# A two-block start pipeline with three gates streamed through one PSUM pool, and pools that wait per tile

## The chip, the cores and the metric

The kernel runs on one core of a Trainium2 chip. The metric is the device time of one execution in microseconds (us); a lower time is better. Before the change, three runs gave 1739.57, 1734.92 and 1736.54 us, the median is 1736.54 us. One further execution was taken with the hardware profiler: it took 1736.99 us, of which the profile's span covers 1735.1 us.

The engines of the core are called PE (matrix multiply), DVE (vector), ACT (scalar, with activation functions) and POOL (general purpose); SP only issues DMAs here. Each engine works through its own instructions in program order. PE writes its results into PSUM, a small memory of eight banks; everything else lives in SBUF.

## What is computed

One layer of a hybrid diffusion backbone, for 640 tokens (128 context and 512 latent tokens), 1024 channels wide:

```python
h    = rms_norm(x) * (1 + scale) + shift        # scale, shift = silu(c) @ w_ada
proj = h @ w_in                                 # q k v | conv b c x | z | xbc | dt | 3 gates
attn = blocked_attention(rope(norm(q)), keys, vals) @ w_attn_o
conv = (conv_bg * dwconv(conv_cg * conv_x, conv_w)) @ w_conv_o
dt   = softplus(dt_raw + dt_bias)
ssd  = ssd_scan(silu(dwconv(xbc)), dt, a) ... @ w_ssd_o
...
y    = x + g1 * ((sigmoid(gate_0) * attn + sigmoid(gate_1) * conv + sigmoid(gate_2) * ssd) @ w_merge)
y    = y + g2 * swiglu(modulated_norm(y))
```

The kernel keeps float32 accuracy with matrix units that take a shorter format: each operand is split into a high part and a low part, and a product is three matmuls, high by high, high by low and low by high.

## The kernel before

**Tiling.** Channels lie on the 128 partitions, so the normalised activations `h` are 8 blocks of 128 x 640, each with a high and a low tile. A matmul takes 320 tokens (half of them) at a time. Weights come in pieces of 128 x 1024 or 128 x 512 float32 (`wr`, three buffers) by DMAs that SP issues. ACT rounds each piece to its high part (`wh`, L166) and DVE subtracts to get the low part (`wl`, L167); `h` is split in the same way.

**Two ways to multiply.** The plain way, `fblock` (L311), costs 3 matmuls for each block of `h`, each half and each 128 output channels: 96 for the 256 output channels of one gate. The other way, `sunit` with `product` (L250), is a seven-product scheme over sums of weight quarters and of `h` quarters: 84 matmuls for the same work, but POOL has to sum weights (`ws`, L227 to L230), DVE has to form sums of `h` quarters once (`sum_forms`, tiles `T`), and DVE and ACT combine the seven products as they come (`uv`, `g`).

**Stages.** The program has these stages, each with a PSUM pool of its own that is opened by `psum(n)`. Here `n` is the count of two-bank accumulators `acc`, and the other banks are single-bank tiles `mx`.

- *Start*, `psum(2)`: load `x`, sum squares (L409), reciprocal root mean square on one row (L359, L346, L348), then a loop over the 8 blocks of `h`. For each block: `products` (16 small matmuls of `silu(c)` with an `ada` weight piece, L419; ACT copies one half of the result as `ms`, L421, and DVE adds the other, L422), `factors` (two tiny matmuls, L428, then shift `mod` and scale `A` on DVE, L429 and L431), `modulated` (the normalised block `hf`, 512 columns on ACT, L435, 128 on DVE, L436, and the high part by an ACT cast, L437), `scaled` (x times the reciprocal root, L440), `low` (L443), and `stream` (12 plain matmuls of the first gate on this block). The loop is a five-step pipeline: step n does products of block n, factors of block n-2, low parts of block n-3 and the gate's matmuls of block n-5. The order of PE, ACT and DVE is the written one here (`manual_schedule`); elsewhere a scheduler orders instructions by priority.
- *Projections and convolution*, `psum(1)`: the four sums of `h` quarters, one plain gate (`plain_gate`, 96 matmuls), the dt matmuls (L499) with which `decays` begins, then four `conv_units` of three seven-product units each, with one seven-product gate after units 1, 2 and 3. `decays` is a generator whose vector work is handed out in pieces between the units: softplus as a polynomial on 128 x 320 tiles (L522 to L529), each step a multiply (L524) and an add (L525).
- *Attention*, `psum(1)` and then `psum(3)` for the scores (L759); *SSD*, `psum(2)`; *merge and FFN*, `psum(4)`, whose second norm starts with a sum of squares `ssq` (L1017) and ten one-column matmuls (L359); *output side of the FFN*, `psum(0)`, which begins with seven-product units again.

**Pools.** When a pool closes and another opens over the same memory, the first writers of the new pool wait until all users of the old one are done.

Of the kernel before, what the change touches and what calls it, by code (L numbers as in the profile page):

```python
# [85 lines left out]
def layer_kernel(  # L86
# [15 lines left out]
    const = ctx.enter_context(tc.tile_pool(name="const", bufs=1))  # L102
    hpool = ctx.enter_context(tc.tile_pool(name="hpool", bufs=2 * KB))
    wp = ctx.enter_context(tc.tile_pool(name="wp", bufs=2))
    fs = ctx.enter_context(tc.tile_pool(name="fs", bufs=8))
# [272 lines left out]
    with tc.tile_pool(name="start", bufs=10) as sp, psum(2):  # L378
# [16 lines left out]
        for k in ORDER[1:3]:  # L395
            modulation_load(k)
# [17 lines left out]
        def products(k):  # L414

            pm, w = mx(), aws.pop(k)
            for i in range(KB):
                q = 32 * (i % 4)
                pe.matmul(pm[q:q + 32, 256 * (i // 4):256 * (i // 4) + 256], cz[:, i, :], w[:, i, :], start=True, stop=True)  # L419
            rows1[k] = sp.tile([P, 256], F32, tag="ms", name=nm("ms"), bufs=4)  # L420
            act.copy(rows1[k], pm[:, :256])  # L421
            dve.tensor_tensor(rows1[k], rows1[k], pm[:, 256:], op=add)  # L422
# [9 lines left out]

        def modulated(k):
# [3 lines left out]
            act.copy(h[k].hi, hf[k])  # L437
# [4 lines left out]
        def low(k):  # L442
            dve.tensor_tensor(h[k].lo, hf[k], f32(h[k].hi), op=sub)  # L443

        def stream(n):
            k = ORDER[n]
            for m in range(2):
                fblock(early[m], we, m, h, k + 1, first=n == 0, last=n == KB - 1, start=k)
# [3 lines left out]
        with tc.manual_schedule(engines={e.engine for e in (pe, act, dve)}):  # L452
            rs = rstd(sq, TOKBLKS, sp)
            for n in range(KB + 5):
                if n + 3 < KB:
                    modulation_load(ORDER[n + 3])
                if n == 0:
                    raws = [qraw(w_gt[EARLY], a) for a in range(2)]
                if n < KB:
                    products(ORDER[n])  # L460
                if n == 0:
                    rr = rowcast(rs, TOKBLKS, sp)
                    early = [acc() for _ in range(2)]
# [1056 lines left out]
```

## Time and profile before

| what | value |
|---|---|
| three runs, median | 1736.54 us |
| the profiled execution | 1736.99 us |
| its span | 1735.1 us |
| granted PE clock, mean over the span | 0.991 |
| PE busy / idle in the span | 1689.1 us / 46.0 us |
| DVE, ACT, POOL busy | 1306.2, 764.8, 297.7 us |

The timeline lists, for each run of like instructions: when it starts in the span, how long it lasts, the engine, the source line, the operation, output tile from input tiles, shapes, and the count; in brackets behind it stand the engine's idle time just before and what ended it. The view of windows gives busy time by engine in a stretch, and then the granted PE clock (1.00 is full, 0.50 is half), the share of DMA time and the rate. PE's matmuls overlap each other a little, so the distance from one start to the next is the cost of one, rather than the listed length.

### The profile page before, as it was taken

The page shows a single profiled execution, that of the slowest core. Times are in us where ns is not written, and L with a number is a line of the kernel's source. Part 1 is how long each engine was busy: PE and PEld are TensorE (multiplying, and loading weights), DVE is VectorE, ACT ScalarE, POOL GpSimd, SP SyncE. Part 2 cuts the span into 40 slices and gives each one's busy share as a digit, 9 for nine tenths or more (in the row PEclk, how much of TensorE's full clock was granted, in tenths as well). Part 3 has the DMA queues.
Part 4 walks back from the last instruction along what each step waited for, and adds up shares of the span by engine and source line. Part 5 has one row for each costly group of instructions (what it writes and reads, how often), then busy time and mean ns, then how long its engine had stood idle before and what let it go on. Part 6 is the DMA issues. An engine that isn't in the chain of part 4 may idle for free.

```text
span 1735.1 us, 30084 instructions
## 1 busy us (share of the span) xinstructions
PE 1689.1 (97%) x11814; PEld 1644.3 (95%) x11814; DVE 1306.2 (75%) x2353; ACT 764.8 (44%) x1437; POOL 297.7 (17%) x261
## 2 busy tenths in 40 slices
PE   5899999999999999999999999999999999999998
PEld 4889999999999999999999999999999999999998
DVE  5799776786646888878877588995578666767888
ACT  4434443565555565555555332312355332424442
POOL 0244451110001111111011000000001231324432
PEclk8999999999999999999999999999999999999999
DMA  8223234211243534454444588773441222222222
GB/s 338 86 82 99 91 123 146 76 44 53 83 125 107 166 123 139 142 161 135 140 150 137 182 284 296 257 231 103 158 145 49 88 73 86 74 86 87 72 74 98
DMA packets 126974, 225.05 MB, mean 130 GB/s; under 512 B 9200, under 2 KB 69488, under 8 KB 125808
## 3 DMA queue, kind: packets, MB, share of 16 engines
q1 hardware_dynamic: 126832, 223.12, 40.1%
q8 instruction: 93, 1.52, 0.4%
q14 instruction: 49, 0.40, 0.1%
HBM read 199.43 MB, written 23.66 MB: 129 GB/s over the span
## 4 chain that ended last, share of the span: by engine, by line
PE 81%; DVE 7%; issue 2%; POOL 1%; ACT 1%; DMA 0%; DVEq 0%; POOLq 0%; ACTq 0%
PE acc L311 41%; PE mx L250 20%; PE mx L311 6%; DVE wl L167 2%; PE acc L1258 2%; PE mx L993 2%; PE mx L945 2%; PE mx L999 1%; PE acc L759 1%; PE mx L298 1%; PE mx L299 1%; PE mx L297 1%; PE mx L971 1%; PE mx L922 1%; PE acc L775 1%
## 5 line engine op out<-in xcount | busy, mean ns | idle before, releaser
L311 PE MATMUL acc<-h,wh 128*128 128x320 f32 x2560 | 488.7, 313 | 1.7 <-DVE h L443 1.0
L311 PEld LDWEIGHTS acc<-h,wh 128*128 128x128 f32 x2560 | 401.0, 189 | 5.1 <-issue 2.7
L166 ACT CAST wh<-wr 128x1024 fp32r<-128x1024 f32 (+2 forms) x224 | 216.7, 969 | 320.7 <-PE acc L311 146.3
L167 DVE TENSOR_TENSOR wl<-wr,wh 128x1024 fp32r<-128x1024 f32 (+2 forms) x224 | 272.8, 1219 | 95.4 <-ACT wh L166 94.1
L311 PE MATMUL acc<-h,wl 128*128 128x320 f32 x1280 | 293.0, 310 | 0.0
L311 PEld LDWEIGHTS acc<-h,wl 128*128 128x128 f32 x1280 | 214.9, 189 | 0.0
L250 PE MATMUL mx<-h,wh 128*128 128x320 f32 x848 | 189.6, 311 | 3.0 <-DVE g L162 3.0
L250 PE MATMUL mx<-s,wh 128*128 128x320 f32 x720 | 160.0, 310 | 0.2 <-DVE s L162 0.2
L311 PE MATMUL acc<-s,wh 128*128 128x320 f32 x768 | 152.7, 309 | 0.0
L967 ACT ACTIVATE ex<-rw,nlc 128x128 f32<-128x128 f32 x320 | 102.7, 394 | 107.3 <-DVE M L969 60.3
L250 PEld LDWEIGHTS mx<-h,wh 128*128 128x128 f32 x848 | 142.4, 189 | 4.1 <-DVE g L162 3.3
L166 ACT CAST wh<-ws 128x512 fp32r<-128x512 f32 (+3 forms) x114 | 84.7, 747 | 132.0 <-PE mx L250 63.8
L961 POOL TENSOR_SCALAR_AFFINE_SELECT rw<-rw 128x512 f32<-128x512 f32 x80 | 57.8, 745 | 463.4 <-DMA rw<-D_a 458.3
L250 PE MATMUL mx<-h,wl 128*128 128x320 f32 x424 | 131.6, 310 | 0.0
L311 PEld LDWEIGHTS acc<-s,wh 128*128 128x128 f32 x768 | 123.1, 188 | 0.3 <-ACT s L169 0.3
L250 PEld LDWEIGHTS mx<-s,wh 128*128 128x128 f32 x720 | 120.7, 188 | 0.7 <-DVE s L162 0.7
L250 PE MATMUL mx<-T,wh 128*128 128x320 f32 x480 | 107.9, 313 | 6.8 <-DVE uv L162 6.8
L167 DVE TENSOR_TENSOR wl<-ws,wh 128x512 fp32r<-128x512 f32 (+3 forms) x114 | 105.7, 928 | 10.7 <-ACT wh L166 9.5
L250 PE MATMUL mx<-s,wl 128*128 128x320 f32 x360 | 111.4, 309 | 0.0
L311 PE MATMUL acc<-s,wl 128*128 128x320 f32 x384 | 97.8, 309 | 0.0
L311 PE MATMUL mx<-s,wh 128*128 128x320 f32 x512 | 95.9, 309 | 0.0
L1117 DVE CUSTOM_DVE_ANT_0 jk<-aw,cr 128x512 f32<-128x512 f32 x128 | 88.2, 689 | 4.5 <-DMA aw<-in_ada_dram 2.1
(306 smaller groups left out, 3268.3 us busy)
## 6 DMA issues: line engine op xcount, KB each, us to landing
wr<-in_w_f_dram SPq DMA_DIRECT2D x60, 512.0 KB, 3.8
rw<-D_a SPq DMA_DIRECT2D x40, 512.0 KB, 3.9
aw<-in_ada_dram SPq DMA_DIRECT2D x64, 256.0 KB, 4.1
wr<-in_w_gt_dram SPq DMA_DIRECT2D x24, 512.0 KB, 3.9
wr<-in_w_cv_dram SPq DMA_DIRECT2D x24, 512.0 KB, 3.9
aw<-in_ada_dram SPq DMA_DIRECT2D x8, 1024.0 KB, 12.6
wr<-in_w_x_dram SPq DMA_DIRECT2D x16, 512.0 KB, 4.0
wr<-in_w_bc_dram SPq DMA_DIRECT2D x16, 512.0 KB, 3.7
```

What stands on the lines that cost most here:

```text
L166: act.copy(hi_t, src)
L167: dve.tensor_tensor(lo_t, src, f32(hi_t), op=sub)
L250: pe.matmul(out, y, z, start=not more and i == 0 and j == 0, stop=i == n - 1 and j == 2, skip_group_check=True)
L297: pe.matmul(out, l.hi, r.hi, start=start, stop=False)
L298: pe.matmul(out, l.hi, r.lo, start=False, stop=False)
L311: pe.matmul(bank(ps, e), x, y[:, e * HT:(e + 1) * HT], start=first and i == start and j == 0, stop=last and i == k - 1 and j == 2)
L945: pe.matmul(ps[:, d0 * GW:d1 * GW], xb[:, c, GW:], xw.pop(c)[:, d0:d1, :], start=True, stop=True)
L961: pool.affine_select(rw[:, d], rw[:, d], pattern=[[0, HPG], [1 - 2 * d, P]], compare_op=ALU.is_ge, fill=-1e4, base=0, channel_multiplier=2 ...
L967: act.activation(ex[:, d, r, :], rw[:, d, r, :], AF.Exp, bias=nlc[:, c, j:j + 1])
L993: pe.matmul(pf[:, q * P:(q + 1) * P], pv[:, c, d, m * P:(m + 1) * P], b["C"][:, tok], start=True, stop=True)
L1117: dve.tensor_tensor_reduce(jk, aw, cr[:, s, :], 0.5, 0.0, op0=mult, op1=add, accum_out=mp[:, q, m, s:s + 1])
L1258: pe.matmul(ps[:, e, :HT], y, z, start=i == 0 and j == 0, stop=i == KB - 1 and j == 2)
```

## The change

It does these things.

1. Every SBUF and PSUM pool is opened with `reuse_waits="tile"`: a new tile waits for the users of its own bytes alone.
2. The pool `psum(1)` is opened once, ahead of the start, and serves the start and the projections. The first gate accumulates in four `mx` tiles, and `products` and `factors` use the other two.
3. The start loop is a two-step pipeline. Step n does the products of block n, the high and low parts of block n-1, `scaled` of block n, the first gate's matmuls of block n-2, and then `factors` of block n, with `hf` in it. The first gate's weights are split in step 1, a second gate's in step 5, and 7 of the 8 blocks of that gate's first half run in steps 7 and 8.
4. `products` accumulates both halves in PSUM, so the eight adds of L422 go.
5. Two gates instead of one are done the plain way, by `streamed`, in the written order, interleaved with the sums of `h` quarters; the written order now reaches to the dt matmuls. Two seven-product gates are left, after units 1 and 3. That is 96 matmuls in place of 84.
6. The two first pieces of gate weights are loaded ahead of the third `ada` piece, and the second gate's pieces in step 1, ahead of `ada` pieces 6 to 8.
7. The polynomial is written so that each step is one `scalar_tensor_tensor`: 9 vector instructions instead of 16.

```diff
-    hpool = ctx.enter_context(tc.tile_pool(name="hpool", bufs=2 * KB))
+    hpool = ctx.enter_context(tc.tile_pool(name="hpool", bufs=2 * KB, reuse_waits="tile"))
...
-        with tc.tile_pool(name=nm("psum"), bufs=2, space=bass.MemoryType.PSUM) as p:
+        with tc.tile_pool(name=nm("psum"), bufs=2, space=bass.MemoryType.PSUM, reuse_waits="tile") as p:
...
-    EARLY, PLAIN, SPARE = GATES[0], GATES[1:2], GATES[5:]
+    EARLY, PLAIN, SPARE = GATES[0], GATES[1:3], GATES[5:]
...
-                pe.matmul(pm[q:q + 32, 256 * (i // 4):256 * (i // 4) + 256], cz[:, i, :], w[:, i, :], start=True, stop=True)
+                pe.matmul(pm[q:q + 32, :256], cz[:, i, :], w[:, i, :], start=i < 4, stop=i >= 4, skip_group_check=True)
             rows1[k] = sp.tile([P, 256], F32, tag="ms", name=nm("ms"), bufs=4)
             act.copy(rows1[k], pm[:, :256])
-            dve.tensor_tensor(rows1[k], rows1[k], pm[:, 256:], op=add)
...
+        rs = rstd(sq, TOKBLKS, sp)
+        early = [(mx(), mx()) for _ in range(2)]
+        fill = None
+        for n in range(KB + 2):
+            if n + 3 < KB:
+                modulation_load(ORDER[n + 3])
+            if n < KB:
+                products(ORDER[n])
+            if n == 0:
+                rr = rowcast(rs, TOKBLKS, sp)
+            if 1 <= n <= KB:
+                parts_of(ORDER[n - 1])
+            if n == 1:
+                we = Quarters([qsplit(raw) for raw in raws])
+                raws = [qraw(w_gt[PLAIN[0]], a) for a in range(2)]
+            if n == 5:
+                wf, fill = Quarters([qsplit(raw) for raw in raws]), acc()
+                raws = [qraw(w_gt[PLAIN[1]], a) for a in range(2)]
+            if n < KB:
+                scaled(ORDER[n])
+            if n >= 2:
+                for m in range(2):
+                    streamed(early[m], we, m, n - 2)
+            if n < KB:
+                factors(ORDER[n])
+            if n == KB - 1:
+                streamed(fill, wf, 0, *range(4))
+            if n == KB:
+                streamed(fill, wf, 0, *range(4, 7))
...
-        dve.tensor_scalar(q, s2, 2.0 / (2 * n + 1), 2.0 / (2 * n - 1), op0=mult, op1=add)
-        for j in range(n - 2, -1, -1):
-            dve.tensor_tensor(q, q, s2, op=mult)
-            dve.tensor_scalar(q, q, 2.0 / (2 * j + 1), None, op0=add)
+        dve.tensor_scalar(q, s2, 2.0 / (2 * n + 1), None, op0=mult)
+        for j in range(n - 1, 0, -1):
+            dve.scalar_tensor_tensor(q, q, 2.0 / (2 * j + 1), s2, op0=add, op1=mult)
             if j % 2 == 0:
                 yield
-        dve.tensor_tensor(q, q, u, op=mult)
+        dve.scalar_tensor_tensor(q, q, 2.0, u, op0=add, op1=mult)
...
+        sums(0)
+        for m in range(2):
+            gate_out(EARLY, m, early[m])
+        streamed(fill, wf, 0, KB - 1)
+        gate_out(PLAIN[0], 0, hv2(fill))
+        sums(1)
+        w3 = Quarters([qsplit(raw) for raw in raws])
+        ps = mx(), mx()
+        streamed(ps, wf, 1, *range(KB))
+        sums(2)
+        gate_out(PLAIN[0], 1, ps)
+        sums(3)
+        for m in range(2):
+            ps = mx(), mx()
+            streamed(ps, w3, m, *range(KB))
+            gate_out(PLAIN[1], m, ps)
+        written.close()
...
-            if i:
+            if i % 2:
                 gate_unit(*todo.pop(0))
```

Three places show how this moves instructions on the engines. A row gives the line, the operation, the output tile from its input tiles (with running numbers) and the shape.

The first place is ACT in the middle of the start loop, around the first split of gate weights. `ms` is the copied result of `products`, `hf` a normalised block, `h` its high part, `wh` the high part of a weight piece. Before:

```order
L421 COPY ms_203<-mx_194 128x256
L421 COPY ms_227<-mx_218 128x256
L421 COPY ms_242<-mx_233 128x256
L435 ACTIVATE hf_104<-s_121,mod_74,A_76 128x512
L437 CAST h_85<-hf_104 128x640
L421 COPY ms_265<-mx_256 128x256
L435 ACTIVATE hf_108<-s_125,mod_74,A_76 128x512
L437 CAST h_93<-hf_108 128x640
L166 CAST wh_278<-wr_190 128x1024
L166 CAST wh_282<-wr_192 128x1024
L421 COPY ms_297<-mx_288 128x256
```

After:

```order
L440 COPY ms_207<-mx_198 128x256
L451 ACTIVATE hf_104<-s_121,mod_74,A_76 128x512
L440 COPY ms_236<-mx_227 128x256
L458 CAST h_85<-hf_104 128x640
L166 CAST wh_240<-wr_143 128x1024
L166 CAST wh_244<-wr_145 128x1024
L451 ACTIVATE hf_108<-s_125,mod_74,A_76 128x512
L440 COPY ms_271<-mx_262 128x256
L458 CAST h_93<-hf_108 128x640
L451 ACTIVATE hf_105<-s_122,mod_74,A_76 128x512
```

The first block's `hf` now comes ahead of the second block's `ms`, the cast of a block comes after the next block's `ms`, and the weight casts follow the first block's cast instead of the second's.

The second place is PE between the last `factors` of the loop and the next group of matmuls. `acc` and `mx` are PSUM tiles, `h` with an odd number is a high part and with an even number a low part, `wh` and `wl` are the weight's parts. Before, the first gate's matmuls of the last two blocks in its stream end the loop, and the plain gate follows in a new pool:

```order
L311 MATMUL acc_215<-h_91,wl_279 128x320 x2
L311 MATMUL acc_214<-h_99,wh_282 128x320 x2
L311 MATMUL acc_214<-h_100,wh_282 128x320 x2
L311 MATMUL acc_214<-h_99,wl_283 128x320 x2
L311 MATMUL acc_215<-h_99,wh_282 128x320 x2
L311 MATMUL acc_215<-h_100,wh_282 128x320 x2
L311 MATMUL acc_215<-h_99,wl_283 128x320 x2
L311 MATMUL mx_600<-h_85,wh_589 128x320
L311 MATMUL mx_601<-h_85,wh_589 128x320
```

After:

```order
L446 MATMUL mx_470<-comb,ms_453 128x2 x2
L311 MATMUL acc_386<-h_85,wh_378 128x320 x2
L311 MATMUL acc_386<-h_86,wh_378 128x320 x2
L311 MATMUL acc_386<-h_85,wl_379 128x320 x2
L311 MATMUL acc_386<-h_93,wh_382 128x320 x2
L311 MATMUL acc_386<-h_94,wh_382 128x320 x2
L311 MATMUL acc_386<-h_93,wl_383 128x320 x2
L311 MATMUL acc_386<-h_87,wh_378 128x320 x2
L311 MATMUL acc_386<-h_88,wh_378 128x320 x2
L311 MATMUL acc_386<-h_87,wl_379 128x320 x2
L311 MATMUL acc_386<-h_95,wh_382 128x320 x2
```

Directly behind the last `factors` there are now matmuls of the second gate on blocks whose parts are early ones, in an accumulator of the same pool.

The third place is PE where the pool `psum(4)` of the merge and FFN gives way to `psum(0)`: `acc_14838` is the last accumulator of the old pool, `mx_14925` and `mx_14926` (after: `mx_14902` and `mx_14903`) are the first two products of the first seven-product unit in the new one, and a bracket names the engines whose semaphores the instruction waits for. Before:

```order
L1258 MATMUL acc_14838<-h_14535,wl_14779 128x320
L250 MATMUL mx_14925<-h_14162,wh_14903 128x320 [waits DVE_49]
L250 MATMUL mx_14925<-h_14162,wh_14903 128x320
L250 MATMUL mx_14925<-h_14162,wl_14904 128x320
L250 MATMUL mx_14925<-h_14174,wh_14903 128x320 x2
...
L250 MATMUL mx_14925<-h_14198,wl_14904 128x320
L250 MATMUL mx_14926<-s_14595,wh_14903 128x320 x2
L250 MATMUL mx_14926<-s_14595,wl_14904 128x320
```

After:

```order
L250 MATMUL mx_14902<-h_14139,wh_14880 128x320 [waits DVE_49]
L250 MATMUL mx_14902<-h_14139,wh_14880 128x320
L250 MATMUL mx_14902<-h_14139,wl_14881 128x320
L250 MATMUL mx_14902<-h_14151,wh_14880 128x320 x2
...
L250 MATMUL mx_14902<-h_14175,wl_14881 128x320
L250 MATMUL mx_14903<-s_14572,wh_14880 128x320 [waits DVE_49]
L250 MATMUL mx_14903<-s_14572,wh_14880 128x320
L250 MATMUL mx_14903<-s_14572,wl_14881 128x320
```

No matmul has moved here, but the waits have: before, the first product waits once, for the last user of the old pool, and the second product has no wait of its own. After, the first product waits for the DVE instructions that read the accumulator whose bytes it takes, the last but one of the old pool, and the second has a wait of its own, for the readers of the last one.

More of the change, by code (lines that the diff above doesn't have):

```diff
@@ L369, in layer_kernel, with streamed, gate_out @@
     GATES = [(br, mt) for br in range(3) for mt in range(4)]
-    EARLY, PLAIN, SPARE = GATES[0], GATES[1:2], GATES[5:]
+    EARLY, PLAIN, SPARE = GATES[0], GATES[1:3], GATES[5:]
     normed = ExitStack()
-    hf_pool = normed.enter_context(tc.tile_pool(name="normed", bufs=KB))
+    hf_pool = normed.enter_context(tc.tile_pool(name="normed", bufs=KB, reuse_waits="tile"))
     hf = [slot(hf_pool, "hf") for _ in range(KB)]
     wdt = hf_pool.tile([P, KB, 64], F32, name="wdt", bufs=1)
-    with tc.tile_pool(name="start", bufs=10) as sp, psum(2):
+    banks, written = ExitStack(), ExitStack()
+    banks.enter_context(psum(1))
+    def streamed(ps, w, m, *ns):
+        for n in ns:
+            k = ORDER[n]
+            fblock(ps, w, m, h, k + 1, first=n == 0, last=n == KB - 1, start=k)
+    def gate_out(x, m, ps):
+        g = slot()
+        for e in range(2):
+            act.activation(g[:, e * HT:(e + 1) * HT], bank(ps, e), AF.Tanh, scale=0.5)
+        nc.sync.dma_start(D_g[KB * x[0] + 2 * x[1] + m], g)
+    with tc.tile_pool(name="start", bufs=10, reuse_waits="tile") as sp:
         cf = sp.tile([P, KB, 2], F32, name="cf", bufs=1)
@@ L394, in layer_kernel @@
         nc.sync.dma_start(par, cols)
-        for k in ORDER[1:3]:
-            modulation_load(k)
+        modulation_load(ORDER[1])
+        raws = [qraw(w_gt[EARLY], a) for a in range(2)]
+        modulation_load(ORDER[2])
         th = sp.tile([P, KB, 2], F32, name="cth", bufs=1)
@@ L436, in modulated, with parts_of @@
             dve.tensor_scalar(hf[k][:, c:c + m], xs[k][:, c:c + m], A1[:, k, 1:2], mod1[:, k, 0, 1:2], op0=mult, op1=add)
-            act.copy(h[k].hi, hf[k])
         def scaled(k):
             dve.tensor_tensor(xs[k], xs[k], rr, op=mult)
-        def low(k):
+        def parts_of(k):
+            act.copy(h[k].hi, hf[k])
             dve.tensor_tensor(h[k].lo, hf[k], f32(h[k].hi), op=sub)
[L445 to L448, printed above, removed]
@@ L452, in layer_kernel @@
[L452 to L463, printed above, removed]
-                if 2 <= n < KB + 2:
-                    factors(ORDER[n - 2])
-                    modulated(ORDER[n - 2])
-                if 1 <= n <= KB:
-                    scaled(ORDER[n - 1])
-                if 3 <= n < KB + 3:
-                    low(ORDER[n - 3])
-                if n == 3:
-                    we = Quarters([qsplit(raw) for raw in raws])
-                if n >= 5:
-                    stream(n - 5)
+        written.enter_context(tc.manual_schedule(engines={e.engine for e in (pe, act, dve)}))
@@ L642, in conv_units, with sums @@
             yield
[L644 to L646 removed]
+        def sums(i):
+            sum_forms(forms, halves, lambda: half_op(pj, "T", 16), (i,))
+        sums(0)
[15 more added lines that the diff above has]
+        written.close()
         todo = [x for x in GATES if x not in [EARLY] + PLAIN + SPARE]
```

40 lines of the change are left out of this document (12 added, 28 removed).

## The prediction

> **What bounds the kernel now.** I read the busy times first, then the chain that ended last, then PE's waits, then PE's timeline around each long wait, and last the windows.
>
> ```profile
> span 1735.1 us, 30084 instructions
> PE 1689.1 (97%) x11814; PEld 1644.3 (95%) x11814; DVE 1306.2 (75%) x2353; ACT 764.8 (44%) x1437; POOL 297.7 (17%) x261
> PE 81%; DVE 7%; issue 2%; POOL 1%; ACT 1%; DMA 0%; DVEq 0%; POOLq 0%; ACTq 0%
> ```
>
> PE is busy for 97% of the span and holds 81% of the chain. It idles 1735.1 - 1689.1 = 46.0 us. So a change that leaves the matmuls alone can win at most these 46 us, and what PE loses at half clock. The first row of PE's waits is the longest.
>
> ```profile
> PE acc L359 <- DVE sq L409: 13.6, 1, 13.6
> ```
>
> 13.6 us pass before the first matmul, and the change touches none of what leads there. The other 32 us lie in the start loop, in the convolution, and where pools close.
>
> ```profile
> 27.97 1.94 PE L419 MATMUL mx<-aw,cz 128*32 128x256 f32 x16 [3.43 <-DMA aw<-in_ada_dram]
> 40.18 1.07 PE L419 MATMUL mx<-aw,cz 128*32 128x256 f32 x16
> 58.27 1.43 PE L311 MATMUL mx<-h,wh 128*128 128x320 f32 x4 [3.68 <-ACT s L478]
> 61.63 1.27 PE L311 MATMUL mx<-h,wh 128*128 128x320 f32 x4
> 73.16 0.75 PE L311 MATMUL mx<-h,wh 128*128 128x320 f32 x4
> 74.04 0.75 PE L311 MATMUL mx<-h,wh 128*128 128x320 f32 x4
> 75.01 4.53 PE L499 MATMUL mx<-hf,wdt 128*64 128x320 f32 x32
> ...
> 26.20:36.45 10.25, 8.48 (x51) 6.01 (x52) 8.84 (x17) 6.82 (x10) 0.00 (x0) 0.50 1.01 407
> 36.45:56.90 20.45, 17.14 (x135) 15.06 (x133) 14.21 (x27) 10.92 (x17) 6.08 (x4) 1.00 0.33 111
> 56.90:63.80 6.90, 5.53 (x21) 5.53 (x22) 6.90 (x11) 3.04 (x6) 2.94 (x2) 0.51 0.45 163
> ```
>
> PE has two prices. From 73.16 to 74.04 six matmuls of 320 columns take 0.88 us, 0.147 each; from 58.27 to 61.63 twelve take 3.36, 0.28 each. The windows give the reason: the granted clock is 1.00 in the one place and 0.51 in the other. A wait of over 3 us here is followed by several us at half clock (3.43 ahead of 27.97, 3.68 ahead of 58.27), so such a wait costs more than its idle time.
>
> **The start, part 1: how fast the new loop can go.** With blocks two steps apart, a block's `hf` follows the block before through ACT and DVE in turn. These rows give the pace (an instruction's cost is the distance to the next start on its engine, about 0.1 us under its length).
>
> ```profile
> 41.32 0.37 ACT L421 COPY ms<-mx 128x256 f32<-128x256 f32 x1 [0.64 <-PE mx L419]
> 42.52 0.82 ACT L435 ACTIVATE hf<-s,mod,A 128x512 f32<-128x512 f32 x1 [0.67 <-DVE A L431]
> 43.23 1.03 ACT L166 CAST wh<-wr 128x1024 fp32r<-128x1024 f32 x1
> 44.17 0.72 ACT L437 CAST h<-hf 128x640 fp32r<-128x640 f32 x1
> ...
> 19.91 0.82 DVE L348 COPY s<-acc 128x640 f32<-128x640 f32 x1 [1.25 <-PE acc L346]
> 42.06 0.15 DVE L429 TENSOR_TENSOR mod<-mx,par 128x4 f32<-128x4 f32 x1
> 42.25 0.23 DVE L431 TENSOR_SCALAR A<-mod,par 128x2 f32<-128x2 f32 x1
> 42.78 0.82 DVE L440 TENSOR_TENSOR s<-s,s 128x640 f32<-128x640 f32 x1
> 43.51 0.82 DVE L443 TENSOR_TENSOR h<-hf,h 128x640 fp32r<-128x640 f32 x1
> 44.30 1.23 DVE L167 TENSOR_TENSOR wl<-wr,wh 128x1024 fp32r<-128x1024 f32 x1
> ```
>
> One block takes `hf` 0.71, the next `ms` 0.27, the cast 0.72, the low part 0.74, `scaled` 0.74, `mod` 0.20, `A` 0.27: 3.67 us with hand-overs. The splits in steps 1 and 5 put two low parts of 1.23 us in front of `scaled`: 6.13 there. The first `hf` can begin after the row at 19.91, one `scaled`, `mod` and `A`: about 22.0. Then 28.1, 31.8, 35.5, 39.1, 45.3, 48.9, 52.6 for the last. PE is to do 1.07 (products) + 12 x 0.147 + 0.5 = 3.33 us per block, which fits in 3.67 at full clock. Eight `ms` adds of DVE are gone. They lay beside PE's work, so I price them at nothing beyond this chain.
>
> **The start, part 2: the matmuls behind it.** The last `factors` needs the `ms` that follows the seventh `hf` on ACT: 48.9 + 0.71 + 0.27, and 0.5 for itself, about 50.5. From there PE has in written order 24 + 12 + 18 + 12 + 6 + 48 + 96 = 216 matmuls (second gate on four blocks, first gate, second gate on three more, first gate, the rest of the second, and the third gate): 216 x 0.147 = 31.7. The cover holds: the last low part is out at 52.6 + 2.2 = 54.8, when PE still has fill until 58. So dt starts at about 82.3, against 75.01 before. But one seven-product gate is gone from the later program, 84 x 0.147 = 12.3 us of PE, and 75.01 + 12.3 = 87.3. The 3.68 us wait with its half clock goes too; that is inside this difference, as are the twelve matmuls more (1.8 us). **The gain is 4.7 to 5.0 at full clock throughout.** The splits leave PE 2.3 to 2.8 us idle in two blocks, and the first blocks run cold as before; I take off 1.5 us and use **3.2 us, from 0 to 5**.
>
> The DMAs moved ahead: the first gate's weights put the third `ada` piece back by 1 MB, at 407 GB/s 2.6 us, to some 23 us, and its user comes at 28. The second gate's weights wait on SP for the split's buffer, and `ada` pieces 6 to 8 are queued behind. The split ends near 27, 1 MB later is 29.3, and the pieces follow each 2.6 us: 32, 34.5, 37, for users after 39. That hides all of it, by over 2 us. The four sums of `h` quarters on DVE now come beside 150 plain matmuls, 22 us; the window from 56.90 shows DVE full for 6.9 us with them, so they fit.
>
> [...]
>
> **The convolution.**
>
> ```profile
> 116.25 0.57 PE L250 MATMUL mx<-T,wh 128*128 128x320 f32 x2 [2.37 <-DVE uv L162]
> 132.28 0.90 PE L250 MATMUL mx<-T,wh 128*128 128x320 f32 x2 [3.35 <-DVE uv L162]
> ...
> 100.00:120.00 20.00, 17.63 (x120) 17.21 (x119) 19.90 (x30) 7.42 (x10) 6.17 (x4) 1.00 0.23 79
> 132.00:135.40 3.40, 3.12 (x12) 3.12 (x13) 3.33 (x8) 0.00 (x0) 0.04 (x1) 0.50 0.46 159
> ...
> 112.22 1.50 DVE L524 TENSOR_TENSOR s<-s,s 128x320 f32<-128x320 f32 x1
> 113.75 0.33 DVE L525 TENSOR_SCALAR s<-s 128x320 f32<-128x320 f32 x1
> ```
>
> Here DVE is the bound: 19.90 of 20.00 us busy, and PE waits for it 2.37 and 3.35 us, then runs 3.4 us at half clock, which costs 1.5. Seven polynomial steps fewer take 0.33 to 1.5 us each off DVE, 2 to 10 us in all. Yet most of those dropped come after the second wait. Ahead of the two waits one step each goes, because each piece between two yields is handed out at a fixed place and the first piece keeps its three steps. The steps that last 1.5 are those beside POOL's weight sums; a shorter list may only move POOL's time to another step. I take **1.0 us, from -1 to 7.2** (2.37 + 3.35 + 1.5, both waits and the clock).
>
> **The pool ends.** Work per pool end: what PE waits for now, and what its new wait is for.
>
> ```profile
> 340.47 0.55 PE L759 MATMUL acc<-kh,qh 128*128 128x320 f32 x2 [1.41 <-ACT raw L713]
> 503.38 0.85 PE L311 MATMUL acc<-h,wh 128*128 128x320 f32 x4 [0.46 <-ACT s L816]
> 994.48 1.30 PE L359 MATMUL acc<-cst,ssq 128*128 128x1 f32 x10 [1.45 <-ACT s L570]
> 1343.27 0.56 PE L250 MATMUL mx<-h,wh 128*128 128x320 f32 x2 [3.00 <-DVE g L162]
> ...
> 995.60:999.00 3.40, 3.40 (x15) 3.40 (x15) 3.01 (x5) 3.21 (x6) 1.67 (x1) 0.50 0.90 300
> 1343.80:1347.20 3.40, 3.40 (x15) 3.40 (x14) 0.00 (x0) 0.42 (x1) 1.72 (x2) 0.50 0.34 131
> ...
> 338.62 0.82 DVE L167 TENSOR_TENSOR ql<-acc,qh 128x640 fp32r<-128x640 f32 x1
> 991.49 1.75 DVE L1017 TENSOR_TENSOR ssq<-ssq,s 128x640 f32<-128x640 f32 x2
> 1337.07 0.87 DVE L162 SCALAR_TENSOR_TENSOR g<-g,acc 128x320 f32<-128x320 f32 x2
> 1342.75 0.47 DVE L162 SCALAR_TENSOR_TENSOR g<-g,acc 128x320 f32<-128x320 f32 x1
> ```
>
> - 340.47: the wait for `raw` on ACT goes; the low part of q, which the scores need, is done at 338.62 + 0.82 = 339.44. Gain **1.0**.
> - 503.38: the wait for `s` on ACT goes, nothing else is late: **0.4**.
> - 994.48: the wait for `s` on ACT goes; `ssq` is done at 993.24, so the start moves 1.2 earlier. The 1.45 us idle and 1.30 us of tiny matmuls are followed by a window at 0.50, where 3.4 us do the work of 1.7. With the idle time gone I count 1.5 of it: **2.7, or 1.2** if the clock falls all the same.
> - 1343.27: PE stands still from 1340.27. The first product, 12 matmuls or 1.76 us, now waits only for a reader that ended at 1337.94, so it runs inside the gap. The second waits until 1342.75 + 0.47 = 1343.22; about 1.2 us idle remains. The window after it was at 0.50: 1.5 more. **3.3, or 1.8** without the clock.
>
> Together **7.4, from 4.4 to 9**. All later users of these pools have waits that are no later than now, so I price the rest at nothing.
>
> **The sum**, against the profiled execution's own time of 1736.99 (0.03% above the median of the runs): 1736.99 - 3.2 - 1.0 - 7.4 = **1725.4 us**, 0.67% faster. A measurement of this kernel can tell about 0.3% from no change, 5.2 us.
>
> **The rivals.**
>
> - *DVE's relief in the convolution counts in full.* For it speaks DVE's 19.90 of 20.00; against it, that few steps go ahead of the waits. Both waits and their clock go: 6.2 us more, 1719.2. Chance 0.17.
> - *The new start gives nothing, or the pools' waits don't fall.* The first: the clock stays low until 36 as before, and the loop wins no time: 1736.99 - 1.0 - 7.4 = 1728.6, less if the clock falls at pool ends all the same: 1731.6. The second, that the option doesn't do what it says: the bracket on the second product speaks against it; then 1736.99 - 4.2 = 1732.8. Chance together 0.22, of which 0.06 lies under 1731.8.
> - *Half clock through the whole start loop: slower.* At half clock a block costs PE 1.93 + 12 x 0.28 + 1.0 = 6.3 us, not 3.67. From the moment PE is the slower of the two, there are no gaps, and the window at 58 to 63 shows that dense work takes some 5 us to come back to full clock; but if the products' small matmuls (32 columns of weights each) don't count as work, it never comes back in the loop. Six blocks by 2.6 is 15.8, and 18 fill matmuls at 0.13 more is 2.4: the start loses 18.2 - 4.7 = 13.5, all else wins 8.4, and the time is 1742. It decides at a granted clock under 3.33 / 3.67 = 0.91 from 26 to 50 us. Against it: the window from 36.45 has 1.00 with the same mix of matmuls. Chance 0.08.
>
> **How the numbers follow.** The forecast has the remaining 0.53. Its own range is 1721 to 1729. Faster by over 0.3% (under 1731.8): forecast 0.53, first rival 0.17, and 0.06 of the second, 0.76 in all. Within 0.3%: 0.16 of the second and 0.03 of the third, 0.19. Slower by over 0.3%: 0.05 of the third. The range runs from 1716, the low ends of all terms, to 1734, above the second rival; it leaves out the third rival and the tails of the terms.
>
> **What would show it.** Right: dt's row at 82 to 84 us; `hf` of the last block near 52; no row with a wait of over 3 us between 26 and 82; PE's clock 1.00 from 36 on; the scores' row without a wait of ACT; the first product of the last pool directly behind the accumulators, and the second behind 1.2 us idle; windows at 1.00 after both pool ends. Wrong: dt later than 87, a window at 0.50 inside the loop, the two `uv` waits as long as now or longer, or gone. A new wait on DVE for the sums of `h` quarters, or on SP's queue for an `ada` piece, would break the cover named in the start.

## The result and the profile after

| kernel | median of the runs | lowest to highest | ratio, 95% interval |
|---|---|---|---|
| before | 1736.6 us (4 runs) | 1734.9 to 1739.6 | |
| changed | 1724.5 us (4 runs) | 1723.1 to 1725.6 | 0.993 [0.9914, 0.9945] |

The changed kernel is 0.7% faster; the forecast was 1725.4 us. The profiled execution took 1725.58 us with a span of 1723.8 us, 11.3 less than before. These lines of the page of the changed kernel answer to those shown of before:

```profile
span 1723.8 us, 30050 instructions
PE 1688.1 (98%) x11826; PEld 1643.1 (95%) x11826; DVE 1295.2 (75%) x2330; ACT 762.5 (44%) x1437; POOL 289.9 (17%) x257
PE 84%; DVE 10%; issue 3%; ACT 1%; DMA 1%; POOL 1%; SPq 0%; DVEq 0%; POOLq 0%; ACTq 0%
```

PE's busy time has hardly moved, though there are 12 matmuls more. Most of the 11.3 us came out of PE's idle time: 1723.8 - 1688.1 = 35.7 us, where it was 46.0. The waits of PE in the changed kernel that bear on the change (each row names the waiting engine and tile, what it waited for, the total, how many times, and the longest):

```profile
PE acc L362 <- DVE sq L428: 13.5, 1, 13.5
PE mx L446 <- ACT ms L440: 4.5, 2, 2.6
PE mx L250 <- DVE uv L162: 4.4, 3, 2.8
PE mx L250 <- DVE g L162: 1.3, 1, 1.3
PE acc L297 <- DVE pTl L167: 1.0, 1, 1.0
```

The wait for `s` where the start's pool ended (3.7 us) is gone, the last pool's wait is 1.3 instead of 3.0, and two waits are new: for `ms` in the start loop, and one of 1.0 us for `pTl` in the attention. The timeline of PE shows where each came. The windows behind it (busy time of PE, of its weight loads PEld, of DVE, ACT and POOL, then the granted clock) show the clock around three of them:

```profile
36.65 0.61 PE L446 MATMUL mx<-comb,ms 128*128 128x2 f32 x4
40.31 0.61 PE L446 MATMUL mx<-comb,ms 128*128 128x2 f32 x4
46.45 0.61 PE L446 MATMUL mx<-comb,ms 128*128 128x2 f32 x4 [2.59 <-ACT ms L440]
...
83.64 4.53 PE L513 MATMUL mx<-hf,wdt 128*64 128x320 f32 x32
...
125.27 0.72 PE L250 MATMUL mx<-T,wh 128*128 128x320 f32 x2 [2.76 <-DVE uv L162]
140.48 0.56 PE L250 MATMUL mx<-T,wh 128*128 128x320 f32 x2 [1.08 <-DVE uv L162]
178.23 0.56 PE L250 MATMUL mx<-T,wh 128*128 128x320 f32 x2 [0.53 <-DVE uv L162]
...
345.52 0.30 PE L297 MATMUL acc<-kh,qh 128*128 128x128 f32 x1 [0.99 <-DVE pTl L167]
...
987.98 1.28 PE L362 MATMUL acc<-cst,ssq 128*128 128x1 f32 x10 [0.25 <-DVE ssq L1036]
...
1335.24 0.56 PE L250 MATMUL mx<-s,wh 128*128 128x320 f32 x2 [1.26 <-DVE g L162]
...
43.59:47.01 3.42, 0.83 (x9) 0.56 (x8) 2.02 (x5) 1.68 (x3) 0.00 (x0) 1.00 0.81 219
47.01:50.42 3.41, 3.41 (x23) 2.14 (x23) 2.21 (x5) 1.45 (x4) 0.00 (x0) 0.50 0.61 227
122.10:125.51 3.41, 0.65 (x4) 0.38 (x3) 3.41 (x7) 0.93 (x1) 0.04 (x1) 1.00 0.00 0
125.51:128.93 3.42, 3.42 (x14) 3.42 (x14) 3.42 (x7) 0.47 (x1) 0.33 (x1) 0.50 0.42 153
987.60:991.00 3.40, 3.15 (x24) 3.02 (x24) 2.77 (x5) 3.40 (x6) 0.70 (x1) 1.00 0.92 305
1335.00:1338.40 3.40, 3.16 (x21) 3.16 (x22) 1.22 (x3) 1.14 (x2) 2.50 (x2) 1.00 0.50 159
```

The reader is to see three things. dt begins at 83.64 us, against 75.01 + 12.3 before: the start won 3.7 us. Behind the second norm and in the last pool the clock is now 1.00, where it was 0.50: there the wait (all of it or most) and the slow stretch behind it went together. And the clock still falls at 47 us and at 125 us. Ahead of the program's end it is at 0.50 in two more stretches, from 23.11 to 29.94 and from 429.30 to 432.71 us. The first of these seems to cost almost nothing: the `factors` in it come 6.18 us behind the ones before them (23.18, 29.36). In experiment 9 below, where PE ran at full pace between the two (16 products in 1.04 us from 22.96, against 1.87 here from 24.12), it is 6.15 us (22.42, 28.57).

Putting like instructions of PE side by side in the two traces gives the shift of the changed kernel by place:

| at (us, before) | shift | so this stage won |
|---|---|---|
| dt, 75.01 (+ 12.3 for the gate) | -3.7 | start: 3.7 |
| first transposes of k, 329.50 | -7.05 | convolution and k, v: 3.4 |
| first scores, 340.47 | -8.02 | pool end: 1.0 |
| next scores, 352.55 | -7.03 | lost again: 1.0 (the wait for `pTl`) |
| 436 to 438 | -5.4 | lost: 1.6 (the stretch at 0.50 from 429.30 us) |
| 504 to 990 | -5.9, then -5.4 | 0.5 won, 0.5 lost |
| behind the second norm, 999 | -8.0 | pool end: 2.6 |
| second product of the last pool, 1346 | -11.0 | pool end: 3.0, and 0.3 more later |

### The profile page after: what moved, and what is told of

Its sections match the earlier page's. It is cut to its first block, busy times and chain, and to the rows that moved or that the text cites. A ratio compares the mean times of both kernels' runs of the same rounds, so it can differ in the third digit from the quotient of the medians.

```text
span 1723.8 us, 30050 instructions
## 1 busy us (share of the span) xinstructions
PE 1688.1 (98%) x11826; PEld 1643.1 (95%) x11826; DVE 1295.2 (75%) x2330; ACT 762.5 (44%) x1437; POOL 289.9 (17%) x257
## 4 chain that ended last, share of the span: by engine, by line
PE 84%; DVE 10%; issue 3%; ACT 1%; DMA 1%; POOL 1%; SPq 0%; DVEq 0%; POOLq 0%; ACTq 0%
PE acc L311 41%; PE mx L250 21%; PE mx L311 7%; DVE wl L167 2%; PE acc L1277 2%; PE mx L1012 2%; PE mx L964 2%; PE mx L1018 1%; PE acc L778 1%; PE mx L298 1%; PE mx L299 1%; PE mx L297 1%; PE mx L990 1%; PE acc L794 1%; PE mx L941 1%
## 5 line engine op out<-in xcount | busy, mean ns | idle before, releaser
L311 PE MATMUL acc<-h,wh 128*128 128x320 f32 x2528 | 480.8, 312 | 0.2 <-ACT s L583 0.2
L311 PEld LDWEIGHTS acc<-h,wh 128*128 128x128 f32 x2528 | 394.8, 188 | 3.2 <-issue 2.7
L311 PE MATMUL acc<-h,wl 128*128 128x320 f32 x1264 | 289.1, 310 | 0.0
L250 PE MATMUL mx<-h,wh 128*128 128x320 f32 x824 | 183.5, 310 | 0.0
L250 PEld LDWEIGHTS mx<-h,wh 128*128 128x128 f32 x824 | 138.0, 188 | 0.7 <-issue 0.5
L250 PE MATMUL mx<-h,wl 128*128 128x320 f32 x412 | 127.3, 309 | 0.0
L167 DVE TENSOR_TENSOR wl<-ws,wh 128x512 fp32r<-128x512 f32 (+3 forms) x111 | 100.2, 904 | 8.3 <-ACT wh L166 7.3
L250 PE MATMUL mx<-T,wh 128*128 128x320 f32 x448 | 100.4, 312 | 4.4 <-DVE uv L162 4.4
## 6 DMA issues: line engine op xcount, KB each, us to landing
aw<-in_ada_dram SPq DMA_DIRECT2D x8, 1024.0 KB, 11.3
```

The lines of the kernel that those rows point to most:

```text
L167: dve.tensor_tensor(lo_t, src, f32(hi_t), op=sub)
L250: pe.matmul(out, y, z, start=not more and i == 0 and j == 0, stop=i == n - 1 and j == 2, skip_group_check=True)
L311: pe.matmul(bank(ps, e), x, y[:, e * HT:(e + 1) * HT], start=first and i == start and j == 0, stop=last and i == k - 1 and j == 2)
```

## The experiments

Each kernel was timed beside the kernel before on one chip. The first three groups ran against medians of before of 1736.8, 1736.4 and 1736.4 us, the last one against 1737.1.

**1. The changed kernel with the old waits.** The option is taken off every pool:

```diff
...
-    hpool = ctx.enter_context(tc.tile_pool(name="hpool", bufs=2 * KB, reuse_waits="tile"))
+    hpool = ctx.enter_context(tc.tile_pool(name="hpool", bufs=2 * KB))
...
```

> The changed kernel with every pool waiting as before (the first part of the change undone, the rest kept). Theory, by the two traces: the pool ends gave 0.4 us at the first group projection, 2.7 at the second norm and 3.3 at the last pool, while the 1.0 won at the first scores was given back 13 us later by a wait for pTl. So 1724.5 + 6.4 = about 1731 us, with the waits of 1.4, 0.5, 1.4 and 3.0 us back in the trace and the first matmul row of dt still near 83.6. Rival: the pools' waits are hidden elsewhere and the start and the polynomial carry the gain: about 1725.

Measured: 1729.78 us, 0.9958 [0.9944, 0.9972]. The waits are back, and dt began at 82.35. PE's waits in this kernel:

```profile
PE mx L250 <- DVE g L162: 3.0, 1, 3.0
PE acc L362 <- ACT s L583: 1.4, 1, 1.4
PE acc L778 <- ACT raw L732: 1.4, 1, 1.4
```

So the option is worth 1729.8 - 1724.5 = 5.3 us here, near the 6.4 expected. dt comes 1.3 us earlier than in the changed kernel, with the same start loop and the same gap: in this execution the clock stayed whole behind it. Timeline and windows of this kernel, to be held against the row at 46.45 and the windows at 43.59 and 47.01 above (the last section has more such pairs):

```profile
46.37 0.61 PE L446 MATMUL mx<-comb,ms 128*128 128x2 f32 x4 [2.58 <-ACT ms L440]
...
42.20:45.62 3.42, 1.59 (x11) 1.32 (x10) 3.32 (x6) 0.87 (x2) 0.00 (x0) 1.00 0.47 102
45.62:49.03 3.41, 2.66 (x27) 2.06 (x28) 1.98 (x5) 1.45 (x4) 0.00 (x0) 1.00 0.91 334
```

**2. The option on the PSUM pools alone.**

> The changed kernel with the per-tile waits on the PSUM pools alone, SBUF pools as before. Theory: all pool ends that PE waits at are PSUM ends, so 1724.5 us, within 1. Rival: a part of the gain comes from SBUF pools (loads and splits that start earlier): between 1726 and 1731.

Measured: 1723.39 us, 0.9923 [0.9911, 0.9935], and PE's instructions stay within 0.4 us of those of the changed kernel. The SBUF pools contribute nothing that can be seen.

**3. The kernel before with the option, nothing else.**

> The kernel before with per-tile waits on all pools and nothing else changed. Theory: the pool ends are worth the same without the new start: 1736.6 - 6.4 = about 1730 us, waits at the second norm near 0.2 us and at the last pool near 1.3; the wait of 3.7 us at 58 us where the start's pool ends goes too or shrinks, which would make it 1727. Rival: they pay only together with the new start: 1736.

Measured: 1728.18 us, 0.9953 [0.9940, 0.9965], 8.6 us better than before. That is more than 5.3: dt begins at 72.96 instead of 75.01, since here the end of the old start stops waiting for ACT too (a wait of 2.39 us for `h` takes the place of the 3.68), and the new start doesn't have that pool end. The rest, 6.5 us, is the same as the 5.3 of the first experiment within what these medians can tell (their intervals are some 2 us to either side).

**4. The start alone**, that is the changed kernel with the old waits and the old polynomial.

> The changed kernel with the old polynomial and pools that wait as before: the start and the plain gates alone. Theory: dt begins at 83.6 us as in the changed kernel, which is 3.7 us better than 75.0 + 12.3 before; 1736.6 - 3.7 = about 1733 us. Rival: the new start needs the per-tile waits, and dt begins at 86 or later: 1735 to 1737.

Measured: 1732.96 us, 0.9977 [0.9967, 0.9986], dt at 83.85. The start is worth 3.8 us and needs no option. In this order the parts are: 1736.76, with the start 1732.96 (-3.8), with the polynomial 1729.78 (-3.2), with the option 1724.50 (-5.3). Such a chain adds up by itself. How far the parts depend on each other is seen in other orders: the option is worth 8.6 us in the kernel before (6.5 without the old start's pool end), and the polynomial 2.5 and 3.9 below. Items 2 to 6 of the change, which make up the start, were only run together, so which of them carries the 3.8 us stays open.

**5. and 6. The polynomial: old in the changed kernel, new in the kernel before.** The edit of the sixth kernel, whose reverse is that of the fifth:

```diff
-        for j in range(n - 2, -1, -1):
-            dve.tensor_tensor(q, q, s2, op=mult)
-            dve.tensor_scalar(q, q, 2.0 / (2 * j + 1), None, op0=add)
+        for j in range(n - 1, 0, -1):
+            dve.scalar_tensor_tensor(q, q, 2.0 / (2 * j + 1), s2, op0=add, op1=mult)
```

> The changed kernel with the old polynomial of 16 vector instructions. Theory: the convolution stage won about 2.9 us between dt and the attention, and the polynomial is why: 1724.5 + 2.9 = 1727.4 us, with waits for uv of 2.4 and 3.4 us again. Rival: that gain comes from the gate that is gone or from the new waits, and the polynomial is hidden: 1724.5, within 1.

> The kernel before with the new polynomial of 9 vector instructions alone. Theory: 1736.6 - 2.9 = 1733.7 us, the second wait for uv falls from 3.4 to about 1.1 us. Rival: it is worth nothing alone, 1736.6, since the first wait stays and the clock still falls.

Measured: 1728.36 us, 0.9952 [0.9940, 0.9965], for the old polynomial in the changed kernel, 3.9 more than the changed one; 1733.83 us, 0.9984 [0.9975, 0.9993], for the new one in the kernel before, 2.5 less. The timeline of the fifth kernel has the second wait as before:

```profile
125.07 0.56 PE L250 MATMUL mx<-T,wh 128*128 128x320 f32 x2 [2.40 <-DVE uv L162]
141.10 0.90 PE L250 MATMUL mx<-T,wh 128*128 128x320 f32 x2 [3.34 <-DVE uv L162]
```

The sixth met its expectation in the time, but not in the wait. The second wait for `uv` was to fall from 3.4 to about 1.1 us; it is 2.64 in this kernel:

```profile
116.50 0.56 PE L250 MATMUL mx<-T,wh 128*128 128x320 f32 x2 [2.76 <-DVE uv L162]
131.72 0.61 PE L250 MATMUL mx<-T,wh 128*128 128x320 f32 x2 [2.64 <-DVE uv L162]
```

The polynomial is the cause of what the convolution won: 2.5 and 3.9 us here, 3.2 between experiments 4 and 1. How it won them is told in the section on the prediction.

**7. The decays' pieces not between the first six units.** What is left in the convolution?

```diff
             for j, _ in enumerate(conv_units(i)):
-                next(dec, None)
+                if i > 1:
+                    next(dec, None)
```

> The changed kernel with the pieces of the decays handed out from the first gate on, none between the first six convolution units. Theory: the two polynomial steps of 1.55 us each that stand ahead of uv at 119 to 122 us are what PE waits for; without them the waits of 2.8 and 1.1 us and the half clock behind the first go: about 1719 to 1721 us. Rival: the convolution's own vector work bounds these units, and the waits stay or move to the later units: 1723 to 1726.

Measured: 1723.54 us, 0.9927 [0.9914, 0.9939]: the rival. The first six units ran without a wait and ended some 6 us ahead of the changed kernel, and then the same vector work made PE wait later, with a slow stretch behind it (0.50 from 201.5 to 204.9 us):

```profile
185.12 0.56 PE L250 MATMUL mx<-T,wh 128*128 128x320 f32 x2 [0.57 <-DVE uv L162]
200.31 0.56 PE L250 MATMUL mx<-T,wh 128*128 128x320 f32 x2 [2.61 <-DVE uv L162]
```

**8. The second gate's split over steps 5 and 6.** Does the gap of 2.59 us bring the half clock at 47 us?

```diff
             if n == 5:
-                wf, fill = Quarters([qsplit(raw) for raw in raws]), acc()
+                wf, fill = Quarters([qsplit(raws[0])]), acc()
+            if n == 6:
+                wf.tiles.append(qsplit(raws[1]))
```

> The changed kernel with the two halves of the second gate's weights split in steps 5 and 6 instead of both in step 5. Theory: the idle 2.6 us of PE at 46 us is what brings the half clock from 47 to 50.5; two gaps of about 1.3 us keep the full clock and dt begins near 82.3 instead of 83.6: about 1723.2 us. Rival: the clock falls all the same (or the chain ends later), dt stays at 83.6 or comes later: 1724.5 to 1726.

Measured: 1724.43 us, 0.9934 [0.9921, 0.9946]; dt at 83.97. The theory that it takes one long gap fell. Timeline and windows of this kernel:

```profile
45.11 0.61 PE L446 MATMUL mx<-comb,ms 128*128 128x2 f32 x4 [1.45 <-ACT ms L440]
50.12 0.61 PE L446 MATMUL mx<-comb,ms 128*128 128x2 f32 x4 [1.45 <-ACT ms L440]
50.59 0.83 PE L311 MATMUL acc<-h,wh 128*128 128x320 f32 x4
...
52.74 1.27 PE L311 MATMUL acc<-h,wh 128*128 128x320 f32 x4
...
41.78:45.20 3.42, 1.97 (x13) 1.71 (x13) 2.49 (x5) 1.21 (x3) 0.00 (x0) 1.00 0.37 69
48.61:52.02 3.41, 1.96 (x15) 1.90 (x15) 1.96 (x6) 1.85 (x4) 0.16 (x1) 1.00 0.48 154
52.02:55.44 3.42, 3.42 (x15) 3.42 (x15) 2.13 (x6) 1.54 (x2) 1.40 (x1) 0.50 0.00 0
```

Behind the first gap of 1.45 us the clock stays whole; behind the second it falls, and the fall shows in the midst of dense matmuls, some 2 us after the gap.

**9. Work put into the gaps.** If the share of work in a stretch counts, filling the gaps must keep the clock. The split goes to steps 4 and 6, and three blocks of the second gate, 18 matmuls, run ahead of the `factors` that PE waits with:

```diff
...
+            if n == 5:
+                streamed(fill, wf, 0, 0, 2)
+            if n == KB - 1:
+                streamed(fill, wf, 0, 4)
             if n < KB:
                 factors(ORDER[n])
             if n == KB - 1:
-                streamed(fill, wf, 0, *range(4))
+                streamed(fill, wf, 0, 1, 3)
             if n == KB:
-                streamed(fill, wf, 0, *range(4, 7))
+                streamed(fill, wf, 0, 5, 6)
```

> The changed kernel with the second gate's weights split in steps 4 and 6 and three of its blocks (18 matmuls) run in front of the sixth and the eighth factors, into the idle time there. Theory: the clock falls in the start where PE has little to do over some 3.4 us, by its share of work and not by one long gap, since with gaps of 1.45 us it fell as well; with 12 and 6 matmuls in those gaps the clock stays at 1.00 from 30 us on, and dt begins near 80 instead of 83.6: 1724.5 - 3.6 = about 1721 us. Rival: it falls all the same (the many small matmuls of the step are what counts as idle), or the sums on DVE become late: dt at 82 to 84, 1723 to 1725.

Measured: 1722.00 us, 0.9920 [0.9906, 0.9934], 2.5 below the changed kernel; dt at 80.42. Of these 3.2 us about 1.3 are the clock: experiment 1, with the gap but with the clock whole behind it, began dt at 82.35. About 1.9 are left for the 18 matmuls in the gaps, whose price is 18 x 0.147 = 2.6 (the start of the whole program also differs by some tenths from execution to execution). The clock is whole from 42 us on:

```profile
80.42 4.53 PE L519 MATMUL mx<-hf,wdt 128*64 128x320 f32 x32
...
42.40:56.00 13.60, 13.60 (x115) 12.40 (x114) 9.01 (x18) 6.27 (x11) 1.60 (x1) 1.00 0.27 89
```

The two later kernels with this edit were at 1.00 from 42 to 56 us as well, while of the seven profiled kernels with the gap of 2.6 us six were not. One point of the expectation was wrong: it had the clock at 1.00 from 30 us on, and behind the gap of 1.87 us at the first split (at 28.57), which this edit leaves, PE ran at half pace: the twelve matmuls from 31.20 us took 3.37 us, the twelve from 36.45 took 1.86.

**10. All of the decays after dt moved behind the last gate**, handed out between the tiles of the k and v projections, where DVE has room:

```diff
...
-        run(heads_norm_rope(wload(w_k), gk, new_k, kraw))
+        for _ in heads_norm_rope(wload(w_k), gk, new_k, kraw):
+            next(dec, None)
...
             split(vv.hi[:, t, :], vv.lo[:, t, :], pq[:, :256])
+            next(dec, None)
```

> The changed kernel with every piece of the decays after dt moved behind the last gate, between the tiles of the k and v projections, where DVE is busy for 5 to 7 of 12 us. Theory: what PE waits for in the convolution is the sum of the decays and the units' own vector work; with the decays out, the waits of 2.8, 1.1 and 0.5 us and the half clock (1.5) go, and nothing comes back: 1724.5 - 5.9 = about 1718.6 us, and no wait for uv over 0.6 us. Rival: they come back in the k and v projections as waits of PE (as they came back in the later units when only the first six were freed): 1721 to 1724.

Measured: 1727.42 us, 0.9951 [0.9938, 0.9963], 2.9 worse than the changed kernel and outside both expectations. The first half of the theory held: the k projection began 9.8 us ahead, at 261.6 us instead of 271.4 (some of it is matmuls that were only moved), with one wait for `uv` of 0.5 us left. Then this row of the timeline gave it back:

```profile
285.01 4.45 PE L552 MATMUL mx<-s,cst 128*128 128x32 f32 x20 [5.84 <-DVE s L546]
```

PE came to the decays' matmuls before DVE's chain of some fifteen steps, one behind the other and between other work, was through. These 20 matmuls themselves then took 4.45 us, and the matmuls of the v projection behind them started 0.21 us apart up to 292 us, and 0.12 us apart from there on.

**11. Experiments 9 and 10 together.**

> Both of the last two edits together. Theory: they lie in different stages and add up: 1724.5 - 5.9 - 3.6 = about 1715 us. Rival: an earlier dt only lengthens a later wait of the convolution for DVE: 1718 or more.

Measured: 1723.74 us, 0.9933 [0.9920, 0.9947]. The rival was right in the number but not in the cause: the wait is again that for `s`, 5.5 us, not one in the convolution.

**12. The same with the decays' matmuls three tiles later.**

```diff
             split(vv.hi[:, t, :], vv.lo[:, t, :], pq[:, :256])
-            next(dec, None)
+            if t > 2:
+                next(dec, None)
```

> As the kernel with both edits, but the decays' matmuls on the cumulative sums come three tiles of the v projection later. Theory: moving the decays frees the convolution of its waits (the trace showed it 9.5 us ahead before the k projection, 5.9 of them matmuls that are only moved), and it was one wait of 5.8 us of PE for the decays' vector chain, with some 2 us at lower clock behind it, that gave it all back. Three tiles of 2.9 us cover that wait: 1723.7 - 5.8 - 2 = about 1716 us and no wait for s over 1 us there. Rival: a wait of the same size turns up at the next matmul that needs the chain, or at the q heads: 1720 to 1724.

Measured: 1713.44 us, 0.9864 [0.9848, 0.9881], 1.4% faster than the kernel before and 11 us faster than the changed one. PE's waits, and the same matmuls in the timeline:

```profile
PE mx L250 <- DVE uv L162: 0.2, 1, 0.2
...
285.12 2.31 PE L558 MATMUL mx<-s,cst 128*128 128x32 f32 x20
```

The decays' matmuls no longer wait for their `s`, the waits for `uv` are down to 0.2 us from 4.4, and the decays' 20 matmuls take 2.31 us instead of 4.45. That is half the time for the same work; the granted clock is 1.00 here from 262 to 300 us. It is the best version here.

## Why the prediction was right, and where its terms were off

The sum was 11.6 us, the measured gain 12.1, and each of the three parts gives a gain by itself. That the sum came so near is in part luck: two of its terms were off by some 2 us each, one low and one high. By its own steps:

- **The start** was put at 3.2 us; it gave 3.7 in the trace and 3.8 alone. The chain of 3.67 us per block was right: between blocks without a split `factors` comes every 3.66 us (36.65, 40.31). With the clock whole, as in experiment 1, dt begins 87.3 - 82.35 = 4.95 us earlier, where 4.7 to 5.0 were reckoned. The fall at 47 us, against the sign "1.00 from 36 on", cost about 1.3 of this, where 1.5 were taken off. Of the two idle times named there, 2.3 to 2.8 us, the one at the second split came as 2.59. At the first split PE ran at 0.50 in the profiled execution and had no idle time (experiment 9 has 1.87 us there); the wait of 1.88 us at 23.18 lies ahead of the split. The last block's `hf` began at 53.66, where 52.6 was reckoned, when PE still had work.
- **The convolution** was put at 1.0 us; the trace gives 3.4 and the polynomial alone 2.5 to 3.9. This is the term that was mis-sized. The step "Ahead of the two waits one step each goes" holds as far as it reaches, and it is worth little. At the first wait the polynomial's work in front of `uv` fell only from 3.2 us (the rest of one step and a whole one) to 3.0 us (two fused steps of 1.5), and a `wl` of 0.6 us now stands ahead of the second `uv`, so that the wait grew from 2.37 to 2.76 us. At the second wait PE goes on 15.2 us behind the first instead of 16.0. What the step left out lies behind the second wait: the slow stretch there, which the 1.0 left as it was, and a third wait for `uv`, which the reckoning does not name (the first row of the block below). Counted from dt, the changed kernel stands 0.4 us ahead at the second wait, 2.1 behind the stretch where before ran at 0.50, 2.9 at the third wait (0.53 us instead of 1.04), and 3.4 at the first transposes of k.
- **Luck in this term.** That the second wait fell to 1.08 us is not the polynomial's doing alone. The clock fell behind the first wait instead, PE came 1.6 us later to the second, and the fall cost nothing, since PE had to wait for `uv` there in any case: in experiment 6, where the clock stayed whole between the two waits, PE goes on after the same 15.2 us, of which it waits 2.64, and then the clock falls (0.50 from 132.1 to 135.5 us). There the polynomial gave 2.5 us, and in the changed kernel more.
- **The pool ends** were put at 7.4 us; taking the option out of the changed kernel costs 5.3. The two large ones came as reckoned: 2.6 at the second norm (2.7), 3.0 to 3.3 in the last pool (3.3), the first product inside the gap and 1.26 us of idle time left (about 1.2). The 1.0 us at the first scores came, too, but was gone 13 us later in the wait for `pTl`: there DVE is busy for 11.74 of 12 us, so that what PE saves it waits for at the next result of DVE. The step that failed is "all later users of these pools have waits that are no later than now": their waits were no later, but DVE was. Of the 2.7 us at the second norm 1.5 were the clock, and this part is not sure either: behind the same wait of 1.45 us PE ran at half pace in experiment 1, too (the six matmuls from 987.61 us took 1.68 us, 0.28 each), while of the two gaps of 1.45 us in experiment 8 only the second was followed by a fall.
- **The rivals.** That DVE's relief would count in full (1719) didn't happen, though more of it counted than I took. That the new start gives nothing is refuted by experiment 4 (3.8 us). That the option would not do what it says is refuted by experiments 1 and 3. The start at half clock throughout is refuted by the window from 36 to 46 us at 1.00. The two errors, 2 us low in the convolution and 2 us high at the pool ends, cancelled.

```profile
172.45 0.56 PE L250 MATMUL mx<-T,wh 128*128 128x320 f32 x2 [1.04 <-DVE uv L162]
110.76 1.42 DVE L525 TENSOR_SCALAR s<-s 128x320 f32<-128x320 f32 x1
115.72 0.48 DVE L162 TENSOR_TENSOR uv<-mx,uv 128x320 f32<-128x320 f32 x1
116.11 0.68 DVE L167 TENSOR_TENSOR wl<-wr,wh 128x512 fp32r<-128x512 f32 x1
...
119.39 3.10 DVE L538 SCALAR_TENSOR_TENSOR s<-s,s 128x320 f32<-128x320 f32 x2
123.07 0.47 DVE L162 TENSOR_TENSOR uv<-uv,mx 128x320 f32<-128x320 f32 x1
124.13 0.68 DVE L167 TENSOR_TENSOR wl<-wr,wh 128x512 fp32r<-128x512 f32 x1
124.73 0.48 DVE L162 TENSOR_TENSOR uv<-mx,uv 128x320 f32<-128x320 f32 x1
...
334.00:346.00 12.00, 11.01 (x89) 10.82 (x88) 11.74 (x28) 6.75 (x22) 1.40 (x2) 1.00 0.27 89
36.00:45.80 9.80, 7.67 (x68) 5.68 (x66) 6.78 (x12) 5.28 (x9) 0.00 (x0) 1.00 0.42 141
```

These lines carry the statements. The first four are of the kernel before: the third wait, the rest of a polynomial step that stood ahead of the first `uv`, and `wl` behind the second `uv`. The others are of the changed kernel: the two polynomial steps ahead of the first `uv` and `wl` ahead of the second in DVE's timeline, and in the windows DVE full behind the first scores and the start loop at full clock from 36 us up to the second split.

What stays open is why the wait for `g` in the last pool could not be made to fall further: the second product takes its bank from the accumulator that is freed last, and a version with another bank was not run.

## What to carry to other kernels

A wait that ends at the close of a pool is worth its idle time, and also the slow stretch behind it if there is one: look at the granted clock behind it (the stretches at 0.50 lasted 3.41 to 10.24 us here). Count the idle time as sure, and the clock only if several executions show the fall, or if the wait is as long as the four of 3.00 to 3.68 us in the kernel before, each of which had one. A wait that goes is won only if the engine behind the next wait isn't full: where DVE is busy for 98% of a stretch, the time comes back a few us later under another name. Vector work that nobody needs soon belongs where the vector engine has room, and the matmul that needs its end must be placed later than the whole chain, which here made the difference between 1723.7 and 1713.4 us.

## What the runs showed of the hardware

In the changed kernel the granted clock is 0.50 from 23.11 to 29.94, from 47.01 to 50.42, from 125.51 to 128.93, from 429.30 to 432.71 and from 1722.95 us to the end of the span. In the kernel before it is 0.50 from 26.21 to 36.45, from 56.93 to 63.76, from 132.02 to 135.44, from 995.60 to 999.01, from 1343.76 to 1347.17 and from 1732.88 us to the end. Between these stretches it is 1.00. Ahead of the end they last 3.41 us, in three places more: 6.83 in two and 10.24 in one.

Waits of PE of like length were followed by such a stretch in one place and not in another. The table has all waits of 1.4 us and more of the kernel before and the changed one, behind the first of the program, and some of the other kernels, each with the start of the row that waited. "Half" and "full" stand where the timeline alone tells, by what a matmul of 320 columns costs: 0.27 us or 0.15.

| idle time of PE | a fall in it or behind it | none |
|---|---|---|
| 3.00 to 3.68 us | before: 3.43 (27.97), 3.68 (58.27), 3.35 (132.28), 3.00 (1343.27); experiment 5: 3.34 (141.10), half | |
| 2.37 to 2.76 us | changed: 2.59 (46.45), 2.76 (125.27); experiments 1, 2 and 8: 2.76 (123.98), 2.75 (125.23), 2.75 (125.59), half; experiments 3 and 4: 2.37 (114.20 and 125.09), half; experiment 6: 2.64 (131.72); experiment 7: 2.61 (200.31) | before: 2.37 (116.25); experiment 1: 2.58 (46.37); experiment 5: 2.40 (125.07), full; experiment 6: 2.76 (116.50) |
| 1.41 to 1.93 us | before: 1.45 (994.48); changed: 1.88 (23.18); experiment 1: 1.45 (986.48), half; experiment 4: 1.93 (141.13), half; experiment 8: 1.45 (50.12); experiment 9: 1.87 (28.57), half | before: 1.41 (340.47); experiment 3: 1.59 (129.91) and 1.51 (143.99), full; experiment 8: 1.45 (45.11); experiment 9: 1.87 (22.42), full |

The wait of 2.76 us in experiment 6 has these windows around it, to be held against the two from 122.10 us of the changed kernel above:

```profile
111.61:115.02 3.41, 2.13 (x15) 1.87 (x13) 3.38 (x5) 2.66 (x4) 1.68 (x2) 1.00 0.01 5
115.02:118.43 3.41, 1.93 (x13) 1.93 (x14) 3.41 (x8) 0.00 (x0) 0.00 (x0) 1.00 0.33 114
```

The stretch from 429.30 us in the changed kernel has no wait of 1 us in the 4 us ahead of it (the longest is 0.8). What decides between the two columns these runs don't show. The length of the wait alone doesn't, and neither does PE's busy time in the window with the gap: in experiment 8 it is 1.97 us in the one window shown and 1.96 us in the other, and only behind the second does the clock fall.

A stretch of 3.41 us at half clock costs up to 1.7 us, an estimate from the matmul's two prices, 0.147 and 0.28 us. The fall at 47 us cost about 1.3, the one at 125 us nothing, as told above. So single executions of like kernels differ by this much, and a term of this size is better read from several runs than from one trace.
